# A four-layer decoder trunk on one core: one-pass matmuls that read the two halves of their moving operand in turn

## The chip, the core and the metric

The kernel runs on one core of a Trainium2 chip, as one program. The metric is the time on the device, in microseconds (us): the median of several executions. All weights, the input and the result are in the device's memory (HBM) before and after; nothing stays on the chip from one execution to the next. In this text PE is the matrix engine (TensorE) and PEld its weight loads, DVE is VectorE, ACT is ScalarE, POOL is GpSimd, and SP the engine that issues most of the DMAs. "L130" is line 130 of the kernel that a profile belongs to.

## The reference

The model has a sequence of 256 tokens with 1024 features and four residual layers: pooling mixer, gated DeltaNet, latent attention (MLA), pooling mixer. All is float32. Shortened:

```python
def reference(x, positions, ...):                  # x: (1, 256, 1024)
    for i in range(4):
        h = rmsnorm(x, norm_g[i])
        y = (pool_mixer, gdn_mixer, mla_mixer)[i % 3](h, ...)
        x = x + y
    return rmsnorm(x, final_g)

def pool_mixer(h, w_in, w_grp, scale, w_out):      # w_in 1024x4096, w_out 2048x1024
    u, gate = jnp.split(h @ w_in, 2, axis=-1)
    # per group: causal mean over a window of 2, 4, 8 or 16 tokens, minus u
    p = einsum('bsgi,gio->bsgo', pooled(u), w_grp)  # 4 groups, 512x512 each
    return (p * scale * silu(gate)) @ w_out

def gdn_mixer(h, w_in, conv_w, ...):               # w_in 1024x6160, w_out 2048x1024
    qkv, gate, b, a = split(h @ w_in)
    q, k, v = split(silu(causal_conv4(qkv)))       # 8 heads, 128 / 128 / 256 wide
    o = chunk_gated_delta_rule(l2norm(q), l2norm(k), v, decay(a), sigmoid(b))
    return (rmsnorm(o) * silu(gate)) @ w_out

def mla_mixer(h, pos, w_in, ...):                  # w_in 1024x3392, w_out 2048x1024
    cq, ckv, k_rope, gate = split(h @ w_in)        # 768, 512, 64, 2048
    q = rmsnorm(cq) @ w_uq                         # 16 heads of 128 + 64 (rotary)
    k_nope, v = split(rmsnorm(ckv) @ w_ukv)        # 16 heads of 128 and 128
    o = causal_softmax_attention(q, k_nope, rope(k_rope), v)
    return (o * silu(gate)) @ w_out
```

Token order matters in four places: the pooling windows and the convolution look back along the tokens, the delta rule and the attention are causal, and the rotary angle is a function of the position. Everywhere else each token is on its own.

## The kernel before

**Precision.** A float32 number is split in two: hi is the number rounded to the one-pass format float32r, lo is what is left. A product of two such numbers is made as three one-pass matmuls, hi·hi, hi·lo and lo·hi, added up in PSUM. Weights are split as they come in (function `weights`, lines 94 to 127): a DMA on SP's queue brings a block, ACT writes hi (L116, or L120 where a gain is multiplied in), and DVE, for some tiles POOL, writes lo = raw - hi (L117, L121). A weight tile is 128 x 512: 128 rows of the contraction by 512 output columns. Tiles lie in a ring of nine. Activations are split in the same manner by `split_out` (L200, L202 on ACT, L205, L207 on DVE).

**Two forms of a projection** (`project`, lines 134 to 191). In the *channel form* (`chan=True`) strips of 128 weight columns stand in the array and the activations of all 256 tokens are the moving operand; the result has channels on partitions and tokens along the free dimension. `mm3` (lines 129 to 132) issues the three matmuls, of 256 columns each: twelve for a weight tile. In the *row form* (`rows`, lines 166 to 174) 128 tokens of the activations stand in the array and the weight tile is the moving operand, 512 columns (320 in one projection of the MLA layer, 256 in the second half of each output projection, where the columns are cut in two); the result has tokens on partitions. That is six matmuls of 512 columns for a tile, or twelve of 256.

The pooling layers use the row form for one gate, one group and the output; the DeltaNet layer for the gates and the output; the MLA layer for the latents, the rotary queries, the values and the output. All else is in the channel form. The row tile t of the residual `xs[t]` has tokens 128t to 128t + 127 on its partitions, in order; PE transposes (through the identity, into PSUM) bring tokens to the free dimension and back.

**Other matmuls.** Transposes, the delta rule's small products, part of the attention scores (the first 128 queries, whose operands are plain float32) and the mask are not in the one-pass format. The attention mask is added by a matmul of a bfloat16 mask with a bfloat16 identity (L1216).

**What sets the order.** The kernel is written on a tile framework, which puts the instructions of each engine in an order by a simulated schedule; `later(...)` holds some back until others are issued. Each engine works its own list from front to back and waits on semaphores. `order` in the DeltaNet layer (line 622) is a list by hand of the steps: the triangular substitution (`s`, POOL, lines 776 to 808) stands ahead of the projections q0, v0, v1, v2, q1, whose matmuls PE has meanwhile.

**Lines the change touches:** `weights`, `mm3`, `project`, `split_out`, the loads of x (L260) and the stores of the result (L389), the pooled split (L508, L509), the query activations (L733), the masks (L567, L1061 to L1065), the positions (L1023), `against` (L756), the turned latents (L1149) and the attention's operands (L1198, L1199, L1219, L1220, L1257, L1260).

## Time and profile before

| | |
|---|---|
| median of 3 executions | 855.13 us (854.04 to 859.54) |
| the profiled execution: time, span | 854.42 us, 852.7 us |
| mean granted TensorE clock | 0.992 |
| PE, DVE, ACT, POOL busy | 835.3, 602.2, 488.7, 155.9 us |
| matmul and weight load records | 5962 each |
| HBM read | 137.27 MB |

The span runs from the first to the last instruction of the profiled execution; its time is 1.7 us longer. Busy time of PE counts a matmul from its start to its modelled end, and matmuls overlap: the mean of 282 ns for 256 columns is how long one is in the array, and the distance from one start to the next is what it costs in a row of them. That distance is read from the order of time. A row of the groups has the line, the engine, the operation, output and inputs, the shape in partitions x elements, the count; then busy us and the mean ns of one; then the idle time just before, and what ended it. In the rows of stretches each engine's busy us stands with the number of its instructions in brackets.

### The profile page before, as it was taken

The numbers are of one execution on the slowest core, as the hardware profiler recorded it, in microseconds if no ns is written. First come the engines' busy times: TensorE is split into PE (matmuls) and PEld (weight loads), VectorE is DVE, ScalarE is ACT, GpSimd is POOL, SyncE is SP. The second block draws the span as 40 slices with busy tenths as digits, with TensorE's granted clock in tenths as the row PEclk, the third lists the DMA queues.
The fourth block names the chain that finished last, engine by engine and source line by source line (L and its number), as shares of the span: only waits on it lengthen the run. The fifth ranks groups of instructions, "written<-read, shape, count | busy, mean of one in ns | idle before, by whom it ended". The sixth has DMA issues, their size and how long they took to land.

```text
span 852.7 us, 16120 instructions
## 1 busy us (share of the span) xinstructions
PE 835.3 (98%) x5962; PEld 778.4 (91%) x5962; DVE 602.2 (71%) x1156; ACT 488.7 (57%) x997; POOL 155.9 (18%) x292
## 2 busy tenths in 40 slices
PE   8999999999999899999999999999999999999997
PEld 7999998988999888788979998999989989999986
DVE  5799986467889976366567649778767568766852
ACT  6655655467746644355565654566555476555642
POOL 3010100224328970032302002000000210000012
PEclk9999999999999999899999999999999999999999
DMA  7666657566665544123557766643652547665661
GB/s 232 199 198 191 181 196 221 149 183 213 173 163 160 156 121 159 36 75 102 171 163 217 201 157 178 192 140 91 170 164 75 173 152 216 180 189 182 184 208 51
DMA packets 108935, 139.90 MB, mean 164 GB/s; under 512 B 21172, under 2 KB 51064, under 8 KB 108856
## 3 DMA queue, kind: packets, MB, share of 16 engines
q1 hardware_dynamic: 106480, 137.12, 53.7%
q0 software_dynamic: 528, 1.58, 0.6%
q8 instruction: 47, 0.77, 0.4%
q10 hardware_dynamic: 1848, 0.17, 0.2%
q14 instruction: 32, 0.26, 0.1%
HBM read 137.27 MB, written 1.58 MB: 163 GB/s over the span
## 4 chain that ended last, share of the span: by engine, by line
PE 68%; POOL 6%; DVE 2%; issue 1%; DMA 1%; ACT 1%; SPq 0%; POOLq 0%; ACTq 0%
PE acc L172 29%; PE acc L130 9%; PE acc L131 9%; PE acc L132 9%; POOL Tb L794 2%; POOL pr L790 2%; PE aux L130 1%; PE aux L131 1%; PE aux L132 1%; PE aux L752 1%; PE aux L923 1%; DMA Lb<-d_l 1%; PE tp L1246 1%; DVE h L346 1%; DVE wlo L117 1%
## 5 line engine op out<-in xcount | busy, mean ns | idle before, releaser
L117 DVE TENSOR_TENSOR wlo<-raw,whi 128x512 fp32r<-128x512 f32 (+1 forms) x430 | 299.0, 719 | 145.7 <-ACT whi L116 143.6
L116 ACT CAST whi<-raw 128x512 fp32r<-128x512 f32 (+1 forms) x444 | 263.2, 617 | 222.6 <-PE acc L172 98.4
L130 PE MATMUL acc<-hTh,whi 128*128 128x256 f32 x832 | 234.4, 282 | 0.9 <-DVE vc L699 0.9
L131 PE MATMUL acc<-hTl,whi 128*128 128x256 f32 x832 | 234.7, 282 | 0.0
L132 PE MATMUL acc<-hTh,wlo 128*128 128x256 f32 x832 | 234.0, 282 | 0.0
L130 PEld LDWEIGHTS acc<-hTh,whi 128*128 128x128 f32 x832 | 156.8, 189 | 1.6 <-DVE vc L699 1.1
L131 PEld LDWEIGHTS acc<-hTl,whi 128*128 128x128 f32 x832 | 156.8, 188 | 0.4
L132 PEld LDWEIGHTS acc<-hTh,wlo 128*128 128x128 f32 x832 | 156.7, 188 | 0.1
L172 PE MATMUL acc<-wlo,yTh 128*128 128x256 f32 (+1 forms) x384 | 116.3, 319 | 0.0
L172 PE MATMUL acc<-whi,yTh 128*128 128x256 f32 (+1 forms) x384 | 116.3, 323 | 0.0
L172 PE MATMUL acc<-whi,yTl 128*128 128x256 f32 (+1 forms) x384 | 92.7, 322 | 0.0
L172 PEld LDWEIGHTS acc<-wlo,yTh 128*128 128x128 f32 x384 | 72.1, 188 | 5.1
L172 PEld LDWEIGHTS acc<-whi,yTh 128*128 128x128 f32 x384 | 71.7, 188 | 5.2
L172 PEld LDWEIGHTS acc<-whi,yTl 128*128 128x128 f32 x384 | 63.2, 188 | 5.5
L120 ACT ACTIVATE whi<-raw,gain 128x512 fp32r<-128x512 f32 x64 | 43.1, 719 | 30.2 <-DMA raw<-in_pool_w_in_dram 22.9
L334 POOL TENSOR_TENSOR hg<-x,gain 128x256 f32<-128x256 f32 x16 | 13.5, 847 | 256.3 <-DVE x L396 254.9
L172 PE MATMUL acc<-wlo,hTh 128*128 128x512 f32 (+1 forms) x144 | 56.4, 396 | 0.3
L121 DVE SCALAR_TENSOR_TENSOR wlo<-raw,gain,whi 128x512 fp32r<-128x512 f32 x64 | 46.8, 746 | 12.6 <-ACT whi L120 12.4
L172 PE MATMUL acc<-whi,hTh 128*128 128x512 f32 (+1 forms) x144 | 54.7, 391 | 0.7 <-ACT hTh L200 0.7
L172 PE MATMUL acc<-whi,hTl 128*128 128x512 f32 (+1 forms) x144 | 44.8, 387 | 0.0
L497 POOL COPY win<-u 128x4 f32<-128x4 f32 x8 | 4.1, 514 | 167.1 <-ACT u L491 93.3
L172 PEld LDWEIGHTS acc<-wlo,hTh 128*128 128x128 f32 x144 | 27.2, 189 | 6.7 <-DVE wlo L117 1.6
(357 smaller groups left out, 1503.0 us busy)
## 6 DMA issues: line engine op xcount, KB each, us to landing
raw<-in_pool_w_in_dram SPq DMA_DIRECT2D x62, 512.0 KB, 4.5
raw<-in_gdn_w_in_dram SPq DMA_DIRECT2D x48, 512.0 KB, 4.2
raw<-in_pool_w_out_dram SPq DMA_DIRECT2D x32, 512.0 KB, 4.3
raw<-in_mla_w_in_dram SPq DMA_DIRECT2D x24, 512.0 KB, 4.3
raw<-in_mla_w_uq_dram SPq DMA_DIRECT2D x36, 256.0 KB, 3.4
raw<-in_pool_w_grp_dram SPq DMA_DIRECT2D x16, 512.0 KB, 3.9
raw<-in_gdn_w_out_dram SPq DMA_DIRECT2D x16, 512.0 KB, 3.8
raw<-in_mla_w_ukv_dram SPq DMA_DIRECT2D x32, 256.0 KB, 3.3
```

The costliest lines, as they stand in the source:

```text
L116: a = nc.scalar.copy(hi, v)
L117: b = e.tensor_tensor(out=lo, in0=v, in1=hi.bitcast(F32), op=ALU.subtract)
L120: a = nc.scalar.activation(hi, v, AF.Copy, scale=g)
L121: b = e.scalar_tensor_tensor(out=lo, in0=v, scalar=g, in1=hi.bitcast(F32), op0=ALU.mult, op1=ALU.subtract)
L130: nc.tensor.matmul(o, lhsT=lhs[0], rhs=rhs[0], start=start, stop=False)
L131: nc.tensor.matmul(o, lhsT=lhs[0], rhs=rhs[1], start=False, stop=False)
L132: return nc.tensor.matmul(o, lhsT=lhs[1], rhs=rhs[0], start=False, stop=stop)
L172: nc.tensor.matmul(o, lhsT=act(k, t * P, P)[x], rhs=parts[j][z][:, sl], start=k == first and x == z == 0, stop=k == last and x == 1)
L334: nc.gpsimd.tensor_tensor(out=self.early[t, a], in0=xs[t][:, sl], in1=self.g[:, sl], op=ALU.mult)
L346: nc.vector.scalar_tensor_tensor(out=h[:, cut:], in0=xs[t][:, sl], scalar=r[:, 0:1], in1=self.g[:, sl], op0=ALU.mult, op1=ALU.mult)
L790: nc.gpsimd.tensor_tensor(out=pv, op=ALU.mult, in0=Lb[:, r, r + 1:, None].to_broadcast([M * Q, n, c]), in1=Tb[:, r:r + 1, :c].to_broadcast ...
L794: mark["blocks"] = nc.gpsimd.tensor_tensor(out=tv, in0=tv, in1=pv, op=ALU.subtract).ins
```

## The change

Each one-pass matmul, and the plain float32 matmuls that share an accumulation or a layout with them, now goes through `mm`. It reads the moving operand as two halves in turn: element 0 of the first half, element 0 of the second, element 1 of the first, and so on. The output is written in order, so the operand has to be stored *woven*: elements 0, 2, 4, ... of what is meant in the first half and 1, 3, 5, ... in the second. The halves are those of each 128 tokens where the moving operand is activations (64 apart), and of the whole width where it is weights (256, 160 or 128 apart). `inorder` and `woven` are two views of the same columns.

```diff
+    def inorder(a, n=P):
+        if len(a.shape) == 3 and a.shape[2] != n:
+            a = a.rearrange("p h s -> p (h s)")
+        if len(a.shape) == 3:
+            return a.rearrange("p h (a b) -> p h a b", b=2)
+        return a.rearrange("p (g a b) -> p g a b", a=n // 2, b=2)
+
+    def woven(a, n=P):
...
+        return a.rearrange("p (g b a) -> p g a b", a=n // 2, b=2)
...
-    def weights(src, n, cols, raw=None, pool=(), gain=None):
+    def weights(src, n, cols, raw=None, pool=(), gain=None, weave=0):
...
+            if weave:
+                v, lo, hi = inorder(v, weave), woven(lo, weave), woven(hi, weave)
...
+    def mm(o, lhs, rhs, start, stop, n=P):
+        return nc.tensor.matmul(inorder(o, n), lhsT=lhs, rhs=woven(rhs, n), start=start,
+                                stop=stop)
+
     def mm3(o, lhs, rhs, start, stop):
-        nc.tensor.matmul(o, lhsT=lhs[0], rhs=rhs[0], start=start, stop=False)
-        nc.tensor.matmul(o, lhsT=lhs[0], rhs=rhs[1], start=False, stop=False)
-        return nc.tensor.matmul(o, lhsT=lhs[1], rhs=rhs[0], start=False, stop=stop)
+        mm(o, lhs[0], rhs[0], start, False)
+        mm(o, lhs[0], rhs[1], False, False)
+        return mm(o, lhs[1], rhs[0], False, stop)
...
+                           weave=0 if chan else cols // cuts)
...
-                        nc.tensor.matmul(o, lhsT=act(k, t * P, P)[x], rhs=parts[j][z][:, sl],
-                                         start=k == first and x == z == 0,
-                                         stop=k == last and x == 1)
+                        mm(o, act(k, t * P, P)[x], parts[j][z][:, sl],
+                           k == first and x == z == 0, k == last and x == 1, width)
...
-    def split_out(*tiles):
+    def split_out(*tiles, weave=False):
+        if weave:
+            tiles = [(inorder(ps), [woven(o) for o in parts], scale)
+                     for ps, parts, scale in tiles]
```

So the weight tiles of the row form are written woven by ACT, DVE and POOL, those of the channel form (they stand in the array) as before. The tokens of a row tile stand on its partitions in the order even, then odd: x is loaded and the result stored so, in two DMAs of 64 rows each where there was one of 128. A transpose then gives activations that are woven already. What is made in the channel form comes out in token order, and is woven when it is split for another channel projection or an output projection (`weave=True` on the pooled activations, the gated pooled products, the attention's queries, keys and outputs).

```diff
+    def by_row(a, t):
+        return a[0, t * P:(t + 1) * P, :].rearrange("(a b) c -> b a c", b=2)
+
     def load_x(t, c):
         sl = slice(c * CW, (c + 1) * CW)
-        nc.sync.dma_start(out=xs[t][:, sl], in_=x[0, t * P:(t + 1) * P, sl])
+        for b in range(2):
+            nc.sync.dma_start(out=xs[t][b * 64:(b + 1) * 64, sl], in_=by_row(x, t)[b, :, sl])
...
-            nc.scalar.copy(phi, p)
-            nc.vector.tensor_tensor(out=plo, in0=p, in1=phi.bitcast(F32), op=ALU.subtract)
+            split_out((p, (phi, plo), None), weave=True)
...
-                                pattern=[[1, P]], channel_multiplier=-1)
+                                pattern=[[1, 2], [2, P // 2]], channel_multiplier=-1)
...
-                    nc.scalar.activation(dst[hf][:, 2 * b + c, :], cv[c], AF.Silu)
+                    o, v = dst[hf][:, 2 * b + c, :], cv[c]
+                    if which:
+                        o, v = woven(o), inorder(v)
+                    nc.scalar.activation(o, v, AF.Silu)
...
+        ckn = Split("ckn", NKV)
...
+                if dst is ckT:
+                    for o, v in zip(ckn.many(a, 2, 0, S), ckT.many(a, 2, 0, S)):
+                        nc.gpsimd.tensor_copy(inorder(o), woven(v.bitcast(F32)))
...
-                        split_out((ps[:, :, a0:], [o[:, two] for o in dst[-1][1]], None))
-                        nc.vector.tensor_copy(dst[-1][0][:, two], ps[:, :, :P])
+                        split_out((ps[:, :, a0:], [o[:, two] for o in dst[-1][1]], None),
+                                  weave=True)
+                        nc.vector.tensor_copy(woven(dst[-1][0][:, two]), inorder(ps[:, :, :P]))
```

The masks, the positions (two DMAs), the decay rows of the delta rule and the identity that adds the attention mask (`turn16`, its columns woven) follow the same order; the values of the MLA layer are projected from a copy of the normalised latents in token order (`ckn`), made by POOL.

The matmuls stand in nearly the same order as before, and as many of them. SP's list begins thus before; `x_93` and `x_94` are the two row tiles, `raw` the buffers for weights:

```order
L260 DMA x_93<-in_x_dram 128x512
L101 DMA raw<-in_pool_w_in_dram 128x512
L260 DMA x_94<-in_x_dram 128x512
L101 DMA raw<-in_pool_w_in_dram 128x512
L260 DMA x_93<-in_x_dram 128x512
L101 DMA raw<-in_pool_w_in_dram 128x512
```

and thus now:

```order
L290 DMA x_93<-in_x_dram 64x512 x2
L117 DMA raw<-in_pool_w_in_dram 128x512
L290 DMA x_94<-in_x_dram 64x512 x2
L117 DMA raw<-in_pool_w_in_dram 128x512 x2
L290 DMA x_93<-in_x_dram 64x512 x2
L117 DMA raw<-in_pool_w_in_dram 128x512
```

Each load of x is two issues, and one weight block has moved ahead of the second half of x. The list ends the same way, with eight stores of 64 rows in place of four of 128. POOL's list in the MLA layer, from the rotary key to the next layer's gain, before:

```order
L1126 TENSOR_TENSOR mrr<-mr,neghalf 128x2
L1096 TENSOR_TENSOR kr<-ra,rb 128x64
L1096 TENSOR_TENSOR qr<-ra,rb 128x512 x4
L334 TENSOR_TENSOR hg<-x_93,gain 128x256
L334 TENSOR_TENSOR hg<-x_94,gain 128x256
```

and now:

```order
L1169 TENSOR_TENSOR mrr<-mr,neghalf 128x2
L1138 TENSOR_TENSOR kr<-ra,rb 128x64
L1197 CAST cknh_6047<-ckTh_6041 128x512
L1197 CAST cknl_6048<-ckTl_6042 128x512
L1197 CAST cknh_6047<-ckTh_6041 128x512
L1197 CAST cknl_6048<-ckTl_6042 128x512
L1138 TENSOR_TENSOR qr<-ra,rb 128x512 x4
L364 TENSOR_TENSOR hg<-x_93,gain 128x256
L364 TENSOR_TENSOR hg<-x_94,gain 128x256
```

The four copies of the latents have come in ahead of the rotary queries (`qr`), which PE transposes.

More of the change, by code (lines that the diff above doesn't have):

```diff
@@ L320, in scales @@
                 nc.vector.tensor_scalar(d, ident, self.r[t], None, ALU.mult)
-                nc.tensor.matmul(ps[:, t * P:(t + 1) * P], lhsT=ones, rhs=d, start=True, stop=True)
+                mm(ps[:, t * P:(t + 1) * P], ones, d, True, True)
             nc.vector.tensor_copy(self.rT, ps[:, :S])
@@ L388, in feed @@
             for c in range(2):
-                nc.sync.dma_start(out=out[0, t * P:(t + 1) * P, c * CW:(c + 1) * CW], in_=y[c])
+                sl = slice(c * CW, (c + 1) * CW)
+                for b in range(2):
+                    nc.sync.dma_start(out=by_row(out, t)[b, :, sl],
+                                      in_=y[c][b * 64:(b + 1) * 64])
     def layer_out(w, yT, ks, i):
@@ L629, in gdn_layer @@
             for x, part in enumerate(hT(k, 0, S)):
-                nc.tensor.matmul(ps[:32, :S], lhsT=bws[:, k].rearrange("p a c -> p (a c)"),
-                                 rhs=part, start=k + x == 0, stop=k == KD - 1 and x == 1)
+                mm(ps[:32, :S], bws[:, k].rearrange("p a c -> p (a c)"), part,
+                   k + x == 0, k == KD - 1 and x == 1)
         ba = workb("ba", S)[:32]
@@ L1022, in rope_tables @@
         posi = const.tile([P, NT], I32, name="posi")
-        nc.scalar.dma_start(out=posi, in_=positions[0].rearrange("(t p) -> p t", p=P))
+        for b in range(2):
+            nc.scalar.dma_start(out=posi[b * 64:(b + 1) * 64],
+                                in_=positions[0].rearrange("(t a b) -> b a t", t=NT, b=2)[b])
         cs = const.tile([P, NT, 2, HALF], F32, name="cs")
@@ L1148, in turned @@
                                             src[t][:, (a + b) * P:(a + b + 1) * P], ident)
-                split_out(*[(ps[:, b * S:(b + 1) * S], dst(a + b, 0, S), col(name, a + b))
-                            for b in range(2)])
+                tiles = [(ps[:, b * S:(b + 1) * S], dst(a + b, 0, S), col(name, a + b))
+                         for b in range(2)]
+                split_out(*tiles)
+                if dst is ckT:
+                    for o, v in zip(ckn.many(a, 2, 0, S), ckT.many(a, 2, 0, S)):
+                        nc.gpsimd.tensor_copy(inorder(o), woven(v.bitcast(F32)))
         turned(cq, NQ, cqT, f"mq{j}")
@@ L1256, in weighted @@
             mm3(po, [a[:, vh] for a in vs], pT, True, False)
[L1257 removed]
+            mm(po[:, P:], v1[:, vh], pT1, False, True)
             y = worka("ym", S)
             nc.vector.tensor_tensor(out=y, in0=po, in1=gs[h // 4][:, h % 4, :], op=ALU.mult)
[L1260 removed]
+            split_out((y, yT(h, 0, S), None), weave=True)
         stages = (scores, flipped, weighted)
```

40 lines of the change are left out of this document (23 added, 17 removed).

## The prediction

> **What bounds the kernel now.** I read the page first, then the groups by shape, then the order of time of single matmuls, the stretches by engine, the waits and the chain that ended last. The page:
>
> ```profile
> span 852.7 us, 16120 instructions
> PE 835.3 (98%) x5962; PEld 778.4 (91%) x5962; DVE 602.2 (71%) x1156; ACT 488.7 (57%) x997; POOL 155.9 (18%) x292
> L116 ACT CAST whi<-raw 128x512 fp32r<-128x512 f32 (+1 forms) x444 | 263.2, 617 | 222.6 <-PE acc L172 98.4
> ```
>
> PE is busy for 98% of the span, and ACT, which makes the weight tiles, waits for PE to give ring buffers back: weights wait for PE, hardly ever PE for weights. So the time is set by how fast matmuls follow each other. A matmul's own duration doesn't tell that, since they overlap; the starts do. First 256 columns in a channel projection (the rows between are the same three lines in turn, sixteen starts in all), then 512 columns in an output projection (nine starts):
>
> ```profile
> 214.20 0.28 PE L132 MATMUL acc<-hTh,wlo 128*128 128x256 f32 x1
> ...
> 215.98 0.28 PE L132 MATMUL acc<-hTh,wlo 128*128 128x256 f32 x1
> ```
> ```profile
> 399.77 0.40 PE L172 MATMUL acc<-wlo,yTh 128*128 128x512 f32 x1
> ...
> 401.63 0.39 PE L172 MATMUL acc<-whi,yTl 128*128 128x512 f32 x1
> ```
>
> 15 steps in 1.78 us are 118.7 ns for 256 columns; 8 steps in 1.86 us are 232.5 ns for 512. Both are about 0.46 ns a column, with no fixed part worth naming. Two other rows show what PE can do at the same granted clock: plain f32 matmuls, and a run of weight loads in front of very short matmuls (64 columns).
>
> ```profile
> 355.51 1.03 PE L950 MATMUL aux<-u,ktok 128*128 128x256 f32 x4
> L950 PE MATMUL aux<-u,ktok 128*128 128x256 f32 x16 | 4.6, 379 | 0.0
> 312.92 1.86 PEld L882 LDWEIGHTS aux<-T,LT 128*128 128x128 f32 x16 [0.29 <-issue]
> ```
>
> The program has 8 matmuls on line 950 and the trace 16 records: a plain f32 matmul is two records. Four records start within 1.03 - 0.38 = 0.65 us, so one takes 217 ns. I read that as each record going over its 256 columns twice, 0.42 ns a column: 8% faster per column than the one-pass matmuls, which have to fetch a new four-byte element for every column. So I take it that the one-pass matmuls are held by the reading of their moving operand, and that is the thing the change alters. The weight loads are the next floor: 16 in 1.86 us, the last of them taking about 0.19 us, make (1.86 - 0.19) / 15 = 111 ns from load to load, and every matmul here has a load of its own (x5962 of both on the page).
>
> **The change part by part.** *The matmuls.* How many are there?
>
> ```profile
> L130 PE MATMUL acc<-hTh,whi 128*128 128x256 f32 x832 | 234.4, 282 | 0.9 <-DVE vc L699 0.9
> L130 PE MATMUL aux<-ph,whi 128*128 128x256 f32 x96 | 26.6, 281 | 0.0
> L130 PE MATMUL acc<-cqTh,whi 128*128 128x256 f32 x64 | 18.4, 287 | 0.0
> L130 PE MATMUL acc<-ckTh,whi 128*128 128x256 f32 x64 | 18.3, 285 | 0.0
> L130 PE MATMUL acc<-cqT,whi 128*128 128x256 f32 x32 | 9.2, 286 | 0.0
> L117 DVE TENSOR_TENSOR wlo<-raw,whi 128x512 fp32r<-128x512 f32 (+1 forms) x430 | 299.0, 719 | 145.7 <-ACT whi L116 143.6
> L121 DVE SCALAR_TENSOR_TENSOR wlo<-raw,gain,whi 128x512 fp32r<-128x512 f32 x64 | 46.8, 746 | 12.6 <-ACT whi L120 12.4
> L117 POOL TENSOR_TENSOR wlo<-raw,whi 128x512 fp32r<-128x512 f32 x14 | 18.5, 1321 | 54.6 <-ACT whi L116 54.5
> L172 PE MATMUL acc<-wlo,yTh 128*128 128x256 f32 x256 | 66.0, 281 | 0.0
> ```
>
> Weight tiles are 430 + 64 + 14 = 508. A channel tile feeds 4 strips x 3 matmuls of 256 columns; line 130 has 832 + 96 + 64 + 64 + 32 = 1088 = 272 x 4, so 272 tiles are channel tiles and 236 row tiles. Of the row tiles 256 x 3 / 12 = 64 run as twelve matmuls of 256 columns (the second output half, cut in two), the rest, about 164 beside eight of 320 columns, as six of 512. If the alternating read brings a column to the 0.42 ns of the plain rows, 512 columns take 217 ns and save 15.5 ns. For 256 columns the load floor ends first: 111 instead of 118.7 saves about 7.2 ns, not 10. Sum: (272 + 64) tiles x 12 x 7.2 ns = 29.0 us, and 164 x 6 x 15.5 ns = 15.3 us: 44 us. The bounds: no gain at all (nothing in this trace reads in such an order), and 57 us where the load floor doesn't hold (12 x 336 x 10.3 ns = 41.5, and 15.3).
>
> *The splits.* ACT and DVE now write the 236 row tiles (6 of them on POOL) with every other element in the other half, and DVE reads whi so too; some 60 splits of activations follow. No row of before shows ACT or DVE hopping at each element. The nearest is the same split without hops, 719 ns, so the lower end is no extra; the upper end is the same split on POOL, 1321 ns, which is 0.60 us more. I take +0.3 us, half way: same engine as the one, more work for its ports as the other. That is 236 x 0.3 = 71 us on DVE and with the activations some 85, almost the same on ACT. [...] Is it hidden? By stretches:
>
> ```profile
> 50.00:100.00 50.00, 50.00 (x402) 48.90 (x401) 46.54 (x87) 29.62 (x50) 5.29 (x5) 1.00 0.62 190
> 250.00:300.00 50.00, 44.34 (x371) 43.35 (x369) 42.83 (x83) 29.58 (x63) 40.36 (x61) 1.00 0.58 173
> 427.00:457.00 30.00, 29.92 (x149) 25.12 (x149) 19.84 (x37) 19.09 (x45) 1.38 (x5) 1.00 0.62 182
> 626.00:686.00 60.00, 59.76 (x421) 54.70 (x419) 39.63 (x100) 32.50 (x90) 7.02 (x13) 1.00 0.41 124
> ```
>
> (After the length: PE, PEld, DVE, ACT, POOL busy, granted clock.) The front of layer 2 (427 to 457, 24 row tiles) would have 19.8 + 7.2 = 27 us of DVE in 28.2 us of PE; its output projections (626 to 686, 32 tiles, 16 head splits) 39.6 + 9.6 + 2 = 51 in 56. Hidden, if thinly. In layer 0 it isn't: 50 to 100 has 46.5 us of DVE already, and with four row tiles and the wider pooled splits (about +3 us) it needs 49.5, while PE would be through in 47. So DVE sets this stretch; over layer 0 I take 4 us of the gain as lost.
>
> *The stretch that follows POOL.* The chain goes through the triangular substitution of layer 1:
>
> ```profile
> 249.57 5.30 DMA Lb<-d_l
> 296.74 0.46 POOL Tb L794
> 300.50 0.69 PE tp L739 x2
> ACT kqT L733 <- POOL pr L790: 5.5, 1, 5.5
> PE tp L739 <- ACT kqT L733: 4.4, 1, 4.4
> ```
>
> From 249.6 to 296.7 DMA and POOL work alone, and PE stands for 4.4 us at the end until the last query tile's buffer is free. PE will only come there sooner: 6% of these 50 us, 3 us, are lost.
>
> *Ends.* Each load of x and each store of the result is now two DMAs.
>
> ```profile
> 1.72 0.42 SPq L260 DMA_DIRECT2D x<-in_x_dram  x1
> 848.98 0.81 SPq L389 DMA_DIRECT2D out_dram<-h  x2
> ```
>
> At 0.4 us an issue, the first half of x is 0.4 us later, and the weight loads queued behind later halves up to 1.7 us; the last row tile's store has two issues more, 0.8 us, with nothing behind them but the end. I take 2 us. The longer split also stands in the way once per layer, where the first row tiles of a layer wait for it: 4 x (0.3 + 0.3), 2 us. The four copies on POOL (the normalised latents in natural order) stand ahead of the rotary sums on a queue that is idle before 514 us; masks, positions and the turned identity are a handful of small instructions, all at nothing.
>
> Sum against the profiled execution, 854.4 us (1.7 over its span, 0.7 under the median of 855.1): 854.4 - 44 + 4 + 3 + 2 + 2 = **821 us**. Own range of this case: 799 with no load floor and hidden splits, 842 with half the gain.
>
> **Rivals.** *The splits eat the gain.* With +0.6 us the front of layer 2 needs 34 us of DVE against 28 of PE, its output stretch 64 against 56, layer 0 another 4, the rest some 7: 25 us lost, about 847. For it: DVE is at 71% and would be at 90% or more of a shorter span. Against: the ring lets DVE run nine tiles ahead. *Reading in turn gains nothing, and the splits are paid.* The 0.46 ns then come from elsewhere; the ends, the heads of the layers and the stretches short of DVE remain: 854 + 2 + 2 + 8 = 866, slower. It decides as soon as the step of a 512-column matmul stays at 232 ns. [...]
>
> **How the numbers follow.** Forecast 0.62; splits eat the gain 0.12; nothing gained 0.12; slower reads 0.14. Range: 797 to 870 takes in the first three and leaves out the last and a few mishaps; the likeliest alone is 799 to 842. A measurement here tells about 1% from no change, 8.5 us. Faster: 0.62 and a third of the 847 case, 0.66; same: the rest of it and a third of the 866 case, 0.12; slower 0.22.
>
> **What would show it.** All one-pass matmuls will stand on one line, that of the new helper. Right: steps of about 111 and 217 ns there; wlo on DVE near 1.0 us for row tiles and 0.72 for channel tiles; 50 to 100 us and 250 to 300 us hardly shorter; PE still over 95%. Wrong: a 256-column step that stays at 118 or passes it; a PE that waits on wlo in the output projections; or a DVE split of 1.3 us, which moves the bound to DVE.

## The result, and the profile after

The changed kernel takes 878.67 us (median of 4, 876.39 to 883.62) where the kernel before takes 855.84 us: 1.027 times as long, 95% interval 1.021 to 1.033. It is slower, and outside the range of the prediction. The page of its profiled execution (880.5 us):

```profile
span 878.7 us, 16173 instructions
PE 820.4 (93%) x5962; PEld 768.5 (87%) x5962; DVE 700.8 (80%) x1156; ACT 605.6 (69%) x997; POOL 168.0 (19%) x296
PE 49%; DVE 16%; DMA 10%; ACT 10%; issue 7%; POOL 6%; SPq 1%; DVEq 0%; ACTq 0%; POOLq 0%
L135 ACT CAST whi<-raw 128x512 fp32r<-128x512 f32 (+1 forms) x444 | 368.5, 903 | 139.2 <-PE acc L148 50.9
L136 DVE TENSOR_TENSOR wlo<-raw,whi 128x512 fp32r<-128x512 f32 (+1 forms) x430 | 385.0, 949 | 90.3 <-ACT whi L135 87.6
```

The third line is the chain that ended last, by engine. PE carries half of it now; DVE, ACT and DMA, through which the weights come, 36%. PE is busy for 15 us less than before and the span is 26 us longer, so PE has 41 us more of waiting. The splits on ACT and DVE have grown by 105 and 86 us of busy time.

Yet the matmuls stepped as forecast. First 512 columns (seven steps; of the rows between, one holds two records), then 256 columns (eleven steps), in order of time:

```profile
535.75 0.38 PE L148 MATMUL acc<-whi,cqTh 128*128 128x512 f32 x1
...
537.26 0.38 PE L148 MATMUL acc<-wlo,cqT 128*128 128x512 f32 x1
```
```profile
500.58 0.28 PE L148 MATMUL acc<-hTl,whi 128*128 128x256 f32 x1
...
501.81 0.28 PE L148 MATMUL acc<-hTh,whi 128*128 128x256 f32 x1
```

1.51 us / 7 = 216 ns, and 1.23 us / 11 = 112 ns (before: 232.5 and 118.7).

Where did the time go? The table compares the same matmuls in each trace, from start to start. The last three columns are experiments told below: e8 reads in turn but writes everything in a run, e13 is the changed kernel with more buffers for raw weights, e14 the kernel before with them.

| stretch, us | before | after | e8 | e13 | e14 |
|---|---|---|---|---|---|
| to the end of the first gate | 20.5 | 22.8 | 22.2 | 22.8 | 20.2 |
| rest of layer 0, output included | 164.9 | 178.9 | 158.6 | 161.9 | 165.1 |
| DeltaNet layer, to the end of its channel stage | 124.5 | 129.3 | 124.8 | 119.9 | 116.3 |
| its late gates and output, the MLA latents | 147.6 | 147.2 | 141.0 | 160.1 | 159.7 |
| MLA gate to queries and values | 158.4 | 150.9 | 150.9 | 150.9 | 158.5 |
| MLA output, layer 3's first gate | 82.3 | 90.4 | 79.5 | 89.6 | 83.0 |
| layer 3 to its last group | 109.2 | 110.1 | 103.0 | 103.2 | 109.4 |
| last output | 38.8 | 41.1 | 36.4 | 37.7 | 38.7 |
| rest of the span | 6.5 | 8.1 | 8.1 | 8.1 | 6.5 |

Only the MLA layer's middle, mostly channel form, keeps the whole gain. The loss lies where row tiles stand: in the output projections and at the heads of the layers behind them. At one such place, the start of layer 0's output, the chain of waits of the changed kernel reads:

```profile
117.31 0.72 DVE wlo L136
118.03 0.02 issue
118.04 5.27 DMA raw<-in_pool_w_out_dram
...
123.39 0.66 DVE wlo L136
124.04 1.20 DVE u L492 x2
125.24 0.98 DVE wlo L136
```
```profile
124.56 0.19 PEld L148 LDWEIGHTS acc<-whi,yTh 128*128 128x128 f32 x1 [2.82 <-ACT whi L135]
126.28 0.79 PE L148 MATMUL acc<-wlo,yTh 128*128 128x512 f32 x1 [1.23 <-DVE wlo L136]
```

DVE ends a split at 118.03; that frees a raw buffer, and 0.01 us later the next block of weights starts to land in it. PE, whose rows follow, stands for 2.8 us until that block is there and split, and again for its low half.

### The profile page after: what moved, and what is told of

Its sections match the earlier page's. It is cut to its first block, busy times and chain, and to the rows that moved or that the text cites. A ratio compares the mean times of both kernels' runs of the same rounds, so it can differ in the third digit from the quotient of the medians.

```text
span 878.7 us, 16173 instructions
## 1 busy us (share of the span) xinstructions
PE 820.4 (93%) x5962; PEld 768.5 (87%) x5962; DVE 700.8 (80%) x1156; ACT 605.6 (69%) x997; POOL 168.0 (19%) x296
## 4 chain that ended last, share of the span: by engine, by line
PE 49%; DVE 16%; DMA 10%; ACT 10%; issue 7%; POOL 6%; SPq 1%; DVEq 0%; ACTq 0%; POOLq 0%
PE acc L148 38%; DVE wlo L136 7%; ACT whi L135 5%; DMA raw<-in_pool_w_out_dram 4%; PE aux L148 4%; DMA raw<-in_pool_w_in_dram 3%; POOL Tb L831 3%; POOL pr L827 2%; DVE wlo L140 1%; DVE win L531 1%; DVE yTl L230 1%; ACT whi L139 1%; ACT ph L225 1%; PE aux L787 1%; ACT junk L239 1%
## 5 line engine op out<-in xcount | busy, mean ns | idle before, releaser
L135 ACT CAST whi<-raw 128x512 fp32r<-128x512 f32 (+1 forms) x444 | 368.5, 903 | 139.2 <-PE acc L148 50.9
L136 DVE TENSOR_TENSOR wlo<-raw,whi 128x512 fp32r<-128x512 f32 (+1 forms) x430 | 385.0, 949 | 90.3 <-ACT whi L135 87.6
L148 PEld LDWEIGHTS acc<-hTh,whi 128*128 128x128 f32 x832 | 162.8, 196 | 4.0 <-ACT gsg L651 2.8
L148 PEld LDWEIGHTS acc<-hTl,whi 128*128 128x128 f32 x832 | 162.7, 196 | 0.3
L148 PEld LDWEIGHTS acc<-hTh,wlo 128*128 128x128 f32 x832 | 162.4, 195 | 0.6 <-DVE wlo L140 0.5
L148 PEld LDWEIGHTS acc<-wlo,yTh 128*128 128x128 f32 x384 | 74.4, 194 | 15.8 <-DVE wlo L136 12.5
L148 PEld LDWEIGHTS acc<-whi,yTh 128*128 128x128 f32 x384 | 74.4, 195 | 9.0 <-ACT whi L135 4.2
L139 ACT ACTIVATE whi<-raw,gain 128x512 fp32r<-128x512 f32 x64 | 47.5, 790 | 28.8 <-DMA raw<-in_pool_w_in_dram 18.5
L140 DVE SCALAR_TENSOR_TENSOR wlo<-raw,gain,whi 128x512 fp32r<-128x512 f32 x64 | 49.5, 800 | 9.9 <-ACT whi L139 9.7
L148 PEld LDWEIGHTS acc<-whi,hTh 128*128 128x128 f32 x144 | 28.1, 195 | 9.9 <-ACT hTh L225 4.4
```

Of the source, the lines that this page charges most:

```text
L135: a = nc.scalar.copy(hi, v)
L136: b = e.tensor_tensor(out=lo, in0=v, in1=hi.bitcast(F32), op=ALU.subtract)
L139: a = nc.scalar.activation(hi, v, AF.Copy, scale=g)
L140: b = e.scalar_tensor_tensor(out=lo, in0=v, scalar=g, in1=hi.bitcast(F32), op0=ALU.mult, op1=ALU.subtract)
L148: return nc.tensor.matmul(inorder(o, n), lhsT=lhs, rhs=woven(rhs, n), start=start, stop=stop)
```

## The experiments

**Whose is the loss?** First the weight splits were taken out of it, keeping TensorE's order of reading (e1); then the hopping writes alone were put into the kernel before (e2).

```diff
# e1: the changed kernel
-            if weave:
-                v, lo, hi = inorder(v, weave), woven(lo, weave), woven(hi, weave)
```


> The changed kernel, but the weight tiles of the row form are split in a run, without hops; PE reads them in turn all the same. What is left out: the columns of the row projections then come out in another order than the reference's, so it is a measurement of time alone. Theory A (the gain at PE is real and the hopping weight splits of 1.17 us on ACT and 1.16 us on DVE eat it): ACT's and DVE's splits back at 0.62 and 0.72 us, steps of 112 and 216 ns, granted clock back at 0.99, time about 822 us (800 to 835). Theory B (PE's turn-wise reading itself makes the stalls, by its collisions or by the clock that is granted): splits may be short, but the clock stays near 0.973 and the time above 860 us. Theory C (the loss comes from woven activations, ends and the other small edits): about 870 us, since those are all still in.

Measured: 837.23 us, ratio to before 0.978 (0.976 to 0.980).

```diff
# e2: the kernel before, row tiles only (n2 is half the width of a matmul)
+                v = v.rearrange("p (g a b) -> p g a b", a=n2, b=2)
+                lo = lo.rearrange("p (g b a) -> p g a b", a=n2, b=2)
+                hi = hi.rearrange("p (g b a) -> p g a b", a=n2, b=2)
```


> The kernel before, with one thing added: the weight tiles of the row form are written with hops as in the change; PE reads and writes as before, so the columns of row projections come out in another order (a measurement of time alone). Theory A: splits of about 1.17 and 1.16 us; the tile pace of PE stays 1.40 us, so a part is hidden; 866 to 890 us, about 875. Theories B and C: within 1% of before, 855 us.

Measured: 878.16 us, ratio 1.026 (1.023 to 1.028). So the way in which ACT and DVE write the row tiles costs 878.7 - 837.2 = 41 us beside the faster PE and 22 us beside the slower one. TensorE's reading is not what loses. e1 stayed 15 us over its expectation: something else takes part of the gain.

**Is the gain in the rows or in the channels?** Row projections read as before, and their tiles are split in a run; only the channel form reads in turn.

```diff
# e3: the changed kernel
-                        mm(o, act(k, t * P, P)[x], parts[j][z][:, sl],
-                           k == first and x == z == 0, k == last and x == 1, width)
+                        nc.tensor.matmul(o, lhsT=act(k, t * P, P)[x], rhs=parts[j][z][:, sl],
+                                         start=k == first and x == z == 0,
+                                         stop=k == last and x == 1)
```


> The changed kernel with the row form put back: weight tiles written in a run and read in a run (233 ns for 512 columns), the channel form and the token order as changed. A correct kernel. Theory A: no hopping weight split left; the channel form keeps 272 x 12 x 6.5 ns = 21 us, of which some 8 are lost beside POOL's chain, in the pooled splits (2.1 us each) and at the ends: about 842 us (832 to 852). Theory B: the channel form's reading in turn stalls as well: over 865 us. Theory C: over 865 us.

Measured: 853.86 us, ratio 0.998 (0.996 to 1.000). Turning the channel form's 272 tiles alone brings next to nothing, 12 us less than the 842 us expected.

**Everything in a run.** Also the activations, woven by ACT and DVE in the changed kernel, are written in a run.

```diff
# e8: e1, and
-        if weave:
-            tiles = [(inorder(ps), [woven(o) for o in parts], scale)
-                     for ps, parts, scale in tiles]
...
-                    if which:
-                        o, v = woven(o), inorder(v)
...
-                        nc.vector.tensor_copy(woven(dst[-1][0][:, two]), inorder(ps[:, :, :P]))
+                        nc.vector.tensor_copy(dst[-1][0][:, two], ps[:, :, :P])
```


> The changed kernel with weight tiles and activations all written in a run, TensorE still reading in turn: no split pays anything, and the kernel computes something else (columns and tokens in another order). It is for the time alone: the PE steps' whole gain, without a price. By the sum of the steps (256 columns 111.7 ns for 118.1, 512 columns 216 for 233, 128 columns of the four-byte kind 136 for 112, all at the granted clock of before) some 811 to 815 us if nothing else binds. If layer 0 and the gated-delta stage are bound by VectorE and GpSimd whatever the splits cost: 828 to 836, near the 837.2 us of weight tiles in a run alone.

Measured: 825.40 us, ratio 0.966 (0.964 to 0.968), between the two expectations. Its page:

```profile
span 824.5 us, 16173 instructions
PE 796.9 (97%) x5962; PEld 756.6 (92%) x5962; DVE 602.2 (73%) x1156; ACT 485.8 (59%) x997; POOL 160.2 (19%) x296
PE 81%; POOL 7%; DVE 5%; DMA 3%; issue 2%; ACT 1%; SPq 0%; POOLq 0%; DVEq 0%; ACTq 0%
```

So reading in turn by itself gains 29.6 us, and the woven activations cost 837.2 - 825.4 = 12 us of it. Ten of these lie in layer 0 (168.7 us in e1 behind the first gate, 158.6 in e8), where the pooled activations are split. That split has nearly doubled; the rows are the changed kernel's, and before the means were 1045 and 1220 ns:

```profile
L225 ACT CAST ph<-p 128x1024 fp32r<-128x1024 f32 x8 | 16.4, 2056 | 5.8 <-DVE p L539 5.7
L230 DVE TENSOR_TENSOR pl<-p,ph 128x1024 fp32r<-128x1024 f32 x8 | 17.2, 2152 | 4.7 <-ACT ph L225 4.7
```

e3 still wrote the activations woven, so those 12 us would explain what it missed; no run shows that apart. A second piece of the missing gain, in e8 as well, is the DeltaNet layer's channel stage. These are that stage before and in e8 (after the length: PE, PEld, DVE, ACT, POOL busy, granted clock, share of the DMA engines, GB/s):

```profile
209.00:310.00 101.00, 94.84 (x790) 93.86 (x790) 88.08 (x186) 64.91 (x131) 62.01 (x83) 0.98 0.55 161
```
```profile
202.00:305.00 103.00, 92.67 (x790) 91.50 (x789) 87.93 (x183) 65.82 (x131) 62.47 (x86) 0.97 0.55 163
```

PE needs 2 us less, DVE's work is the same 88 us, and the stage is 2 us longer: it isn't PE that sets it. What does was not tested.

**Which engine's split?** Only the high half (ACT) hops, then only the low half (DVE).

```diff
# e5: the changed kernel
-                v, lo, hi = inorder(v, weave), woven(lo, weave), woven(hi, weave)
+                hi = woven(hi, weave)
+                v, lo = inorder(v, weave), inorder(lo, weave)
# e6: the changed kernel
-                v, lo, hi = inorder(v, weave), woven(lo, weave), woven(hi, weave)
+                lo = woven(lo, weave)
+                v, hi = inorder(v, weave), inorder(hi, weave)
```


> The changed kernel, but of a row projection's weight tile only the high half (ScalarE) is written hopping; VectorE reads that half hopping and writes the low half in a run, so the two halves disagree in the order of their columns and the kernel computes something else; it is for the time alone. Known: both halves hopping 878.7 us, neither 837.2 us. If the loss comes by ScalarE's longer split (1.17 us in place of 0.62, and the matmuls wait for the first half): 865 to 880. If it comes by VectorE (80% busy, 0.45 us more in each split): 837 to 850, with VectorE's split back near 0.75 us. If it is the length of the way from landing to both halves, on which the two add: about 860. The lengths are to show first whether a hopping read costs VectorE anything.

> The changed kernel, but only the low half (VectorE, and GpSimd's few) is written hopping; ScalarE writes the high half in a run. The halves disagree in the order of their columns, so it computes something else; it is for the time alone. If the loss comes by ScalarE: 837 to 850. If by VectorE: 865 to 880. If by the sum of both on the way of a tile: about 858. VectorE's split should stay near 1.16 us, ScalarE's go back to 0.62 us.

Measured: e5 854.07 us, 0.999 (0.997 to 1.000); e6 853.81 us, 0.999 (0.997 to 1.001). The groups of e5, then of e6:

```profile
L136 ACT CAST whi<-raw 128x512 fp32r<-128x512 f32 (+1 forms) x444 | 361.5, 884 | 127.4 <-PE acc L149 52.2
L137 DVE TENSOR_TENSOR wlo<-raw,whi 128x512 fp32r<-128x512 f32 (+1 forms) x430 | 301.0, 720 | 129.8 <-ACT whi L136 128.0
```
```profile
L137 DVE TENSOR_TENSOR wlo<-raw,whi 128x512 fp32r<-128x512 f32 (+1 forms) x430 | 374.3, 922 | 72.8 <-ACT whi L136 69.7
L136 ACT CAST whi<-raw 128x512 fp32r<-128x512 f32 (+1 forms) x444 | 260.1, 619 | 190.6 <-PE acc L149 76.5
```

Neither engine alone is the cause: each half costs 17 us over e1, both cost 41, 7 more than the two together. Both times lie nearest to the third branch of their expectations (about 860 and 858). And DVE pays for the write, not for the read: with a hopping source and a result in a run it stays at 720 ns.

**Turned round: read at a step of two, write in a run.** The same data in the same places; only the order in which ACT and DVE go through them is another.

```diff
# e4: the changed kernel, weight tiles only; e7: the same in split_out, queries and keys too
-                v, lo, hi = inorder(v, weave), woven(lo, weave), woven(hi, weave)
+                v = v.rearrange("p (g a b) -> p g b a", a=weave // 2, b=2)
+                lo, hi = (a.rearrange("p (g b a) -> p g b a", a=weave // 2, b=2)
+                          for a in (lo, hi))
```


> The changed kernel with one loop order altered: ACT and DVE go over a row tile in the order in which it is stored, so they read raw at a step of two elements and write hi and lo in a run; what is stored is the same, and the kernel is correct. Theory A with hops at the write as the price: splits near 0.7 us and 825 us. Theory A with any step as the price: splits stay near 1.15 us and the time near 878 us. Between them if only DVE or only ACT gains. Theories B and C: about 878 us.

> The changed kernel with all of its woven writes on ScalarE and VectorE (weights and activations: pooled values, gated outputs, keys, queries) turned round: the source is read at a step of two and the result is written in a run; it computes the same as the reference. Beside it stand 840.2 us with the weight tiles alone so. If the woven activations cost layer 0 and the gated-delta layer their gain (the pooled split took 2.06 and 2.15 us where it had 1.05 and 1.22): 828 to 834, with the pooled split at 1.3 to 1.5 us and the stretch 119 to 132 us 3 to 5 us shorter than in the changed kernel. If not: 838 to 842.

Measured: e4 840.18 us, 0.982 (0.979 to 0.986); e7 832.64 us, 0.975 (0.972 to 0.977). Both are faster than the kernel before and than the changed one, and compute the same. e4 is 15 us over its 825, as e1 was over its 822: both still write the activations hopping. The pooled split of e7:

```profile
L241 ACT CAST ph<-p 128x1024 fp32r<-128x1024 f32 x8 | 11.1, 1390 | 4.4 <-DVE p L555 4.4
L246 DVE TENSOR_TENSOR pl<-p,ph 128x1024 fp32r<-128x1024 f32 x8 | 11.3, 1408 | 1.9 <-ACT ph L241 1.9
```

**Through what do longer splits act?** The page of the changed kernel gives the time from issue to landing, median, in its list of transfers:

```profile
raw<-in_pool_w_in_dram SPq DMA_DIRECT2D x62, 512.0 KB, 4.3
```

With that, two splits of about 1.17 us on ACT and the last of 1.15 us on DVE, a raw buffer comes free again after 4.3 + 2.3 + 1.15 = 7.8 us. There are three, each with two row tiles: one row tile in 1.30 us, and PE needs 6 x 216 ns = 1.30 us for it. Before, with the landing of that kernel's page, the sum was 4.5 + 1.24 + 0.72 = 6.5 us, a tile in 1.08 us beside PE's 1.40. That is an estimate, and it says only that the changed kernel has no room left; five raw buffers test it, and more buffers for finished halves test the rival, that the reserve of split tiles is too small.

```diff
# e9: the changed kernel; e11: e7
-    rawp = ctx.enter_context(tc.tile_pool(name="rawp", bufs=3))
+    rawp = ctx.enter_context(tc.tile_pool(name="rawp", bufs=5))
# e10: the changed kernel
-    ring = ctx.enter_context(tc.tile_pool(name="ring", bufs=9))
+    ring = ctx.enter_context(tc.tile_pool(name="ring", bufs=11))
```


> The changed kernel (878.7 us) with five buffers for the raw weights as they land, in place of three: same instructions, more loaded ahead. If what binds is the round trip of a raw buffer (landing 4.3 us, then two splits of 1.17 us each on ScalarE and the last one's 1.16 us on VectorE, for two row tiles: about 8 us by three buffers, 1.33 us a row tile beside TensorE's 1.30): 850 to 860, and ScalarE's waits for a landed weight fall to a few us. If it is the time of the splits themselves on ScalarE and VectorE, which a loaded-ahead buffer doesn't shorten: 874 to 880.

> The changed kernel with eleven buffers for each half of the split weight tiles in place of nine. If TensorE runs dry because the reserve of split tiles is used up at a layer's end and refilled slowly (1.17 us for a split beside 1.30 for its use, so that a tile of reserve takes some nine tiles to win back), two more tiles give at most 2 x 1.3 us at each of the some eight places that lose: 862 to 874. If the reserve never fills at all because the splits are too slow on the whole: 876 to 880.

> The kernel with all woven writes turned round (read at a step of two, written in a run: 832.6 us) and five raw buffers. If landings still hold splits up here: 826 to 830. If not: 831 to 834.

Measured: e9 853.28 us, 0.998 (0.997 to 1.000): 25 us came back. e10 898.62 us, 1.051 (1.047 to 1.056). e11 836.93 us, 0.979 (0.976 to 0.982). e9 speaks for the round trip, but the buffers also let the scheduler move work: in e9 the stretches outside the DeltaNet layer are 29 us shorter, and inside it 4 us are lost. e10 missed both expectations. Its order moved most in the DeltaNet layer, whose channel stage is 15 us shorter and whose late gates are 27 us longer, and at several other places it lost or won 2 to 4 us; it tells nothing sure of the reserve. e11 lost 15 us in the late gates too.

So the buffers were made deeper outside the DeltaNet layer only, in the changed kernel, in the kernel before and in e7.

```diff
# e13: the changed kernel; e14: the kernel before; e15: e7
+            at = deep["at"] if deep["on"] else 0
+            deep["at"] = (at + 1) % 5
-            raw = rawp.tile([P, KU * CW], F32, tag="raw", name="raw")
+            raw = rawp.tile([P, KU * CW], F32, tag="raw" if at < 3 else "rawx", name="raw",
+                            bufs=3 if at < 3 else 2)
...
+        deep["on"] = i % 3 != 1
```


> The changed kernel with five raw buffers outside the gated-delta layer, and three in it as before. With five everywhere (853.3 us) the stretches outside that layer were 32 us shorter, its channel stage 10 us shorter and its output stage 15 us longer. If the round trip of a raw buffer (landing, ScalarE's split, VectorE's split) is what the hopping splits stretched, the 32 us come and the layer stays as it was: 845 to 855. If the gain of the five came through the order in the gated-delta layer: 870 to 880.

> The kernel before with the same five raw buffers outside the gated-delta layer. If the round trip binds only where the splits hop: 851 to 856, no change. If the raw buffers bound the kernel before as well: 835 to 848, and then the price of the hopping splits is smaller than the comparison of e9 made it.

> The kernel with all woven writes turned round (832.6 us), with five raw buffers outside the gated-delta layer. With five everywhere (836.9 us) the stages ahead of that layer were 4.1 us shorter, its two stages together 8.7 us longer, and nothing else moved. If it is the layer's order alone that lost there: 827 to 830. If the deeper buffers ahead of it move the layer too: 832 to 838.

Measured: e13 858.27 us, 1.003 (1.001 to 1.005); e14 861.33 us, 1.008 (1.004 to 1.011); e15 833.23 us, 0.973 (0.970 to 0.977). The expectations failed in one thing, that the DeltaNet layer would stay as it was: what is loaded ahead of it moved its order all the same (the table: its channel stage 8 to 9 us shorter, what follows 12 to 13 us longer, in the changed kernel and in the one before; in e15 8 and 15). Why that layer loses on balance was not pursued. Outside it the trace decides: e13 is 28 us shorter than the changed kernel, e14 within 1 us of the kernel before, e15 6 us shorter than e7. So the raw buffers bound the changed kernel, e7 a little, and the kernel before not at all. The windows of layer 0 behind its first gate, first of the changed kernel, then of e13, and then the same for what follows layer 3's first gate, up to the last matmul:

```profile
22.80:201.70 178.90, 164.87 (x1225) 154.17 (x1225) 149.04 (x221) 119.51 (x165) 24.21 (x29) 0.96 0.58 175
22.80:184.70 161.90, 156.75 (x1226) 149.09 (x1225) 147.87 (x220) 119.54 (x165) 27.29 (x30) 1.00 0.63 195
```
```profile
719.50:870.60 151.10, 144.63 (x1135) 139.32 (x1133) 118.45 (x152) 99.14 (x140) 11.34 (x20) 0.98 0.55 174
705.20:846.10 140.90, 140.18 (x1135) 136.21 (x1133) 118.71 (x153) 101.54 (x140) 13.32 (x20) 1.00 0.56 180
```

DVE and ACT do the same work in less time, so neither was full. In layer 0 the order of DVE's list has moved with the buffers as well, and that share can't be told apart. In the second pair the lists of PE, DVE, ACT and POOL have the same instructions in the same order, but for one matmul at the border: these 10 us come from the buffers and not from another order. The waits in layer 0, first the changed kernel from 22 to 202 us, then e13, then the kernel before over the same work (after the colon: us in total, times, longest us):

```profile
ACT whi L139 <- DMA raw<-in_pool_w_in_dram: 16.8, 14, 3.2
PEld acc L148 <- DVE wlo L136: 7.6, 9, 1.5
ACT whi L135 <- DMA raw<-in_pool_w_out_dram: 5.6, 5, 2.4
```
```profile
ACT whi L143 <- PE acc L152: 10.6, 13, 1.6
PEld acc L152 <- DVE wlo L140: 1.5, 2, 1.0
```
```profile
ACT whi L120 <- DMA raw<-in_pool_w_in_dram: 20.2, 15, 2.5
PEld acc L172 <- DVE wlo L117: 0.6, 1, 0.6
```

With five buffers ACT waits for PE in place of landings. But ACT's wait for landings is not the sign by itself: the kernel before has 20.2 us of it, and its PE hardly waits. The sign is that PE runs dry behind it, 7.6 us on DVE's splits in the changed kernel.

**How far does the sum go?** By it e2 (1.3 us a tile beside 1.40), e5 (1.23 beside 1.30) and e6 (1.12 beside 1.30) have room and should lose nothing; they lost 22, 17 and 17 us. The same two stretches, in us, from their traces:

| stretch | before | e2 | e1 | e5 | e6 | after | e13 |
|---|---|---|---|---|---|---|---|
| layer 0 behind its first gate | 164.9 | 172.4 | 168.7 | 173.2 | 173.6 | 178.9 | 161.9 |
| behind layer 3's first gate, to the last matmul | 148.0 | 148.0 | 141.5 | 141.6 | 143.6 | 151.1 | 140.9 |

At the end of the kernel the sum holds, save for 2 us of e6: e2 and e5 lose nothing there, and only the changed kernel, which has no room, loses 10. In layer 0 it doesn't: with room left, e2 loses 7.5 us beside the kernel before, and e5 and e6 lose 4.5 and 4.9 us beside e1. There splits also stand behind other work in DVE's list (in the chain above, 1.20 us of `u` between two splits); that this is the reason is not shown.

Nor are the raw buffers all. Outside the DeltaNet layer the changed kernel lies 44 us over e8, and e13 still 16 us, 10 of them in the MLA output, which deeper buffers leave at 89.6 us. That stretch in the changed kernel, then in e8:

```profile
629.10:719.50 90.40, 83.40 (x541) 74.37 (x540) 73.72 (x135) 67.37 (x126) 8.27 (x14) 0.98 0.41 127
```
```profile
597.50:677.00 79.50, 78.73 (x540) 72.82 (x539) 56.39 (x133) 48.55 (x124) 7.89 (x14) 1.00 0.44 138
```

DVE and ACT do 17 and 19 us more there and the stretch is 11 us longer, though both have idle time left. The attention heads stand in the same queues; I take it that splits and heads delay each other, but no run separates that.

**A last variant.** In e12, on top of e7, the output projections' tiles are split straight through, and the 24 additions to x read their sums at a step of two.

```diff
# e12: e7; run=True goes to the two output projections
-            nc.vector.tensor_tensor(out=xv, in0=ps, in1=xv, op=ALU.add)
+            v = inhalves(xv, n)
+            nc.vector.tensor_tensor(out=v, in0=bytwos(ps, n), in1=v, op=ALU.add)
...
-                           weave=0 if chan else cols // cuts)
+                           weave=0 if chan or run else cols // cuts)
```


> The kernel with all woven writes turned round (832.6 us), and of the output projections (128 of the some 240 row tiles) the weight tiles split straight through, with nothing at a step; instead the 24 additions to x read their sums at a step of two, so that the columns come out in order and it computes the same as the reference. Half of the 3 us that lie between weight tiles at a step of two and in a run (840.2 and 837.2 us) is 1.5 us; 24 additions longer by 0.1 to 0.2 us each cost VectorE 2 to 5 us, of which the last of each layer lies on the path. So 830 to 834: 830 if the splits' length still counts, 834 if the ends of the layers count more.

Measured: 832.46 us, 0.974 (0.971 to 0.978), the same as e7 within the measurement. e7, e12 and e15 can't be told apart; e7 is the simplest, 7 us over e8.

## Why the prediction was wrong

**Right: what bounds the kernel, and the step of the matmuls.** 111 and 217 ns were forecast, 112 and 216 were measured, and the rivals that deny the gain have fallen: with all writes in a run (e8) reading in turn gives 0.966. An operand read from two halves in turn was the faster of the two here: 216 ns against 232.5 for 512 columns, 112 against 118.7 for 256. Why it is, no run shows: that a plain float32 record goes over its columns twice, and that the reading of the operand holds the one-pass matmuls, was my inference from the 217 ns.

**Too large: the sum of the steps.** 44 us less the 4, 3 and 2 us for layer 0, POOL's stretch and the ends is 35 us; e8, which pays no hopping write, gained 29.6. The three lost terms were the right ones, two of them too small. Layer 0 behind its first gate gained 6.3 us in e8 where its steps alone make an estimated 10 (1006 matmuls x 7 ns and 172 x 16.5 ns), so 3.5 us are lost and 4 were booked. The DeltaNet channel stage loses its whole gain (672 matmuls x 7 ns = 4.7 us) and 1.8 us more, where 3 us were booked. (That DMA and POOL "work alone" there holds for the chain only: by the row of 250 to 300 us PE is busy for 44.3 of the 50.) The start and the end cost 1.7 + 1.6 us where 2 were booked. One cost was not seen at all: the plain float32 matmuls of 128 columns got slower, below.

**Mis-sized: the price of a hopping split.** +0.3 us was taken, half way between the same split in a run and the split on POOL. The rows of the result give, for ACT, (903 - 617) x 444 / 228 = 557 ns, and for DVE, (949 - 719) x 430 / 222 = 445 ns, over the hopping tiles alone (236, less 8 that take the gain, and for DVE less 6 on POOL). The upper end of the bound, 0.60, was the nearer. These are lengths, and neighbours overlap: in busy time DVE took 99 us more over the whole kernel and ACT 117, where 85 were booked for each. On DVE it is the hopping result, not the hopping source, that costs anything here: in e5, with a hopping source and a result in a run, its split took 720 ns, against 719 before.

**The step that failed: "hidden, if thinly".** Cover was counted as busy time of an engine in a stretch: 51 us of DVE in 56 of PE. By that sum even +0.6 us gave only 847, the first rival; the time came out 32 us over that, with DVE at 80%. No engine was full: in layer 0 DVE was busy for 149 us of 179, and e13 did the same work in 162. What ended the cover, for 28 us, was the way of one block: landing, ACT, ACT, DVE, and only then the buffer for the next. Three splits grew on it at once, three buffers were all there was, and PE had become faster. e13 beside e14 (28 us back, and none) shows that, most plainly behind layer 3's first gate, where 10 us came back with the order of the work unchanged. "The ring lets DVE run nine tiles ahead" stood against the first rival; the raw buffers ahead of the ring were not counted.

The size of the price alone doesn't repair the forecast. With its own +0.3 us the same sum would have been 4.3 + 1.84 + 1.02 = 7.2 us, 1.19 us a tile beside PE's 1.30, with +0.6 us 8.1 us and 1.34; so +0.3 would have passed by this sum too, and e5, e6 and e2 lost time in layer 0 with room left. Of the 53 us between the changed kernel and e8, 28 go with the raw buffers. Of the other 25, 10 lie in the MLA output, 11 in the DeltaNet layer and the latents behind it; how the splits act there stays open.

**Of the signs that were named:** the steps came as said; wlo of the row tiles was to be near 1.0 us and was 719 + 445 = 1164 ns (949 is the mean of hopping and other tiles), between that and the 1.3 us that was to show a wrong forecast; 50 to 100 and 250 to 300 us got no gain; "a PE that waits on wlo in the output projections" was named as the sign of a wrong forecast, and it came. "PE still over 95%" did not: 93%.

## What to carry to other kernels

Here a layout that brought the consumer from 232.5 to 216 ns for 512 columns was paid by those who write it, with 557 ns a tile on ACT and 445 on DVE. Before counting such a price as hidden, add up the whole way of one block (landing, each split, the release of its buffer), divide it by the number of buffers, and compare that with the consumer's new pace, not only with an engine's busy share. Leave room in it: where the same engines have other work in their lists, time was lost here at 1.12 and 1.23 us a tile beside 1.30. Where a copy has to reorder, let it read at a step and write in a run rather than the other way round: here that turned a loss of 2.7% into a gain of 2.5%. And when buffers are added on a framework that schedules, look which other work moves before crediting the buffers.

## What the runs showed of the hardware that was not expected

ACT pays most for a hopping write: 557 ns more on 128 x 512 elements, where DVE pays 445. Read at a step of two and written in a run, the same tiles cost little: in e4 the groups' means are

```profile
L137 ACT CAST whi<-raw 128x512 fp32r<-128x512 f32 x436 | 292.1, 714 | 157.2 <-PE acc L150 60.7 <-DMA raw<-in_gdn_w_in_dram 20.5 <-DMA raw<-in_pool_w_in_dram 17.7
L138 DVE TENSOR_TENSOR wlo<-raw,whi 128x512 fp32r<-128x512 f32 x422 | 306.5, 756 | 101.9 <-ACT whi L137 99.1 <-PE acc L150 1.9
```

against 620 and 723 before in the same groups, which over the tiles concerned is 0.19 us on ACT and 0.07 us on DVE.

Reading in turn helped the one-pass matmuls (512 columns from 232.5 to 216 ns, 256 columns from 118.7 to 112). Plain float32 ones of 128 columns, each two records here, became slower; first before, then after:

```profile
642.55 0.38 PE L1219 MATMUL aux<-qk,qk 128*128 128x128 f32 x2
642.77 0.39 PE L1220 MATMUL aux<-krT,qr 128*128 128x128 f32 x2
```
```profile
650.61 0.44 PE L148 MATMUL aux<-qk,qk 128*128 128x128 f32 x2
650.88 0.43 PE L148 MATMUL aux<-krT,qr 128*128 128x128 f32 x2
```

0.22 us for two records, 110 ns each, became 0.27 us, 135 ns each.

Behind its long waits PE had a lower granted clock here. Behind the wait at 126.28 us, shown above, and a little later in the changed kernel:

```profile
126.86 1.06 PE L148 MATMUL acc<-whi,yTh 128*128 128x512 f32 x2
127.72 1.47 PE L148 MATMUL acc<-wlo,yTh 128*128 128x512 f32 x2
...
132.15 0.38 PE L148 MATMUL acc<-wlo,yTh 128*128 128x512 f32 x1
132.37 0.38 PE L148 MATMUL acc<-whi,yTh 128*128 128x512 f32 x1
```
```profile
125.20:131.80 6.60, 5.49 (x12) 3.95 (x13) 6.60 (x10) 4.43 (x5) 0.86 (x1) 0.50 0.47 156
```

Two matmuls of 512 columns take 0.86 us, 430 ns each, and some 5 us later 220 ns each; between 125.2 and 131.8 us the granted clock was 0.50. Over the 1.5 us behind each of PE's six waits of 2 us or longer in that trace it was 0.50 to 0.68, and 0.50 behind the one of 4.4 us in the kernel before; in the changed kernel it was 1.00 behind eight of the ten shorter waits over 1 us. That the wait is the cause is inferred from this; no run varies it alone. The mean granted clock over the span fell from 0.992 to 0.973, which is 0.027 x 878.7 = 24 us of full clock withheld against 7 us before; in e8 it is 0.990, 8 us. So of the 54 us by which the changed kernel's span exceeds that of e8, 31 are idle time of PE and 23 longer busy time for the same matmuls (820.4 and 796.9 us), and withheld clock accounts for at most 16 of the 23. What the waits would have cost without it was not measured.
